# Eighth input block split first, the last blocks' final additions placed between root steps, and a fourth input tile, in a hybrid attention layer

## The chip, the cores and the metric

The kernel runs on one core of a Trainium2 chip. The core has a matmul engine (TensorE, PE in the profile, with PEld for its weight loads), VectorE (DVE), ScalarE (ACT), GpSimd (POOL) and SyncE (SP); each takes its instructions in one fixed order and waits where an instruction's inputs or its output's space aren't ready. SP and POOL mainly issue DMAs here. The metric is the device time of one execution in microseconds (us).

## The reference

One layer over 1024 tokens of width 1024: a normed projection into queries, keys, values and gates, two kinds of attention, a mix, and a gated MLP, each with a residual.

```python
h = rms_norm(x, pre_mix_g)
proj = h @ w_in                      # q, k, v of two attentions, gates
...                                  # differential and dilated attention
mix = (g_a * ya + g_b * yb) @ w_mix_out
x = x + rms_norm(mix, post_mix_g)
h = rms_norm(x, pre_ffn_g)
u = causal_depthwise_conv(h @ w_up, conv_w, conv_b)
gate, val = jnp.split(u, 2, axis=-1)
y = (gelu(gate) * val) @ w_down
x = x + rms_norm(y, post_ffn_g)
```

Everything is float32. Only the very first stage (the value columns of `proj`) and the very last (the product with `w_down`, its norm and the residual) are touched by the change.

## The kernel before, in words

**Precision.** A float32 operand is held as a high and a low part (`whi`/`wlo` for weights, `xh`/`xl` for x): ACT writes the high part, DVE subtracts it from the source to get the low part (L146, L367), and `mm3` makes three matmuls (L155 to L157), high by high, high by low, low by high.

**The first stage (values).** The products of x by the value weights `w_v` are computed by a Strassen-like scheme with seven products per half of the columns, named p1 to p7, each over four k steps and four token blocks of 128. Its operands are blocks of x^T and sums of such blocks. x^T comes in eight tiles `xt` of 128 x 1024, in the order `K_FIRST = (4, 0, 5, 1, 6, 2, 7, 3)`; the pool has six buffers for them (`XT_BUFS`), so the seventh (`xt_245`) and the eighth tile (`xt_256`, rows K = 3) can be loaded only when the first tiles are done with. `split_x` (L369) splits one half of a tile: ACT writes `xh` (L371), DVE `xl`. `sums_x(k, low, high)` (L374) makes the sum operands t1 to t4 of one k from two tiles: some seven ACT and ten DVE steps, among them the last reader of a tile, the DVE step that writes `cos` (L367; the sums are formed in the buffers called `sin` and `cos`). `sums_x(0)` and `sums_x(1)` are called in the loop over the tiles after j = 5 and j = 7, `sums_x(2)` after the loop, `sums_x(3)` after the first eight steps of the product. `ready_v(n)` splits the weights of a step n, `step_v(n)` issues its matmuls, and after a product's last k step `take_v` (L490) evacuates the four accumulators, some of them by an ACT copy to `yv` (L505). The next product in the same banks can start only after that.

**The norm's rows.** From step 14 on `norm_x` (L397) loads the eight row blocks of x by POOL (`rows`, L404, 512 KB each) into four big buffers, tagged `kk`, `ang`, `sin`, `cos` in turn, and sums their squares by ACT (L401, one step of 128 x 1024, in place). The third block (`rows_670`) takes the `sin` buffer, which `sums_x(3)` has used before: its last reader there is the DVE step `t3l<-sin`, so POOL's load waits for that.

**The order.** The program is traced, and a scheduler fixes each engine's order ahead of time by its own model of costs and by priorities: `tc.high_priority(offset)` moves work forward, `tc.issue_after(ins)` keeps what is traced inside it behind an instruction on its engine, without a wait.

**The last stage.** The last product, p4 of the product with `w_down`, is made in two ways: its first four of eleven f steps go over all four token blocks, then each block m finishes its last seven by itself (L1680 on), so that PE ends the blocks one after the other. While it does, `finish` (L1617) normalises and adds the first four row blocks (tile `x2` of 128 x 1024 from `x2_d`, L1607, then DVE L1619 and L1620, then the output DMA). After each block m of the second four come: `take` (DVE, L329, from the accumulator), `sum_squares` (ACT, L1603), a product with gpost (DVE, L1686, in place, so it waits for the square to have read), `rsqrt_row` (L183: DVE `r1v`, ACT square root `r1y`, then four small DVE steps with `r1w` as the result), and for each half a DVE step L1689, `x2 = y * r + x2`, and an output DMA. The tile `x2` has three buffers: its eight loads go over SP's queue, and the fourth and later ones wait for an earlier output DMA.

Of the kernel before, what the change touches and what calls it, by code (L numbers as in the profile page):

```python
# [15 lines left out]
F32 = mybir.dt.float32  # L16
# [3 lines left out]
ALU = mybir.AluOpType  # L20
# [67 lines left out]
def trunk(ctx: ExitStack, tc: tile.TileContext, a, out):  # L88
# [90 lines left out]
        nc.vector.tensor_scalar(y, y, 1.0 / f, None, op0=ALU.mult)  # L179
        return y  # L180

    def rsqrt_row(x, y):

        v, r, w = (tiny.tile([P, 1], F32, tag="r1" + c, name="r1" + c) for c in "vyw")
        if y is None:
            nc.vector.tensor_scalar(v, x, EPS * D, None, op0=ALU.add)
        else:
            nc.vector.tensor_scalar(v, x, y, EPS * D, op0=ALU.add, op1=ALU.add)
        nc.scalar.activation(r, v, AF.Sqrt, scale=1.0 / D)
        nc.vector.reciprocal(r, r)  # L190

        nc.vector.tensor_scalar(w, r, r, v, op0=ALU.mult, op1=ALU.mult)
        nc.vector.tensor_scalar(w, w, -3.0 * D, r, op0=ALU.add, op1=ALU.mult)
        return w
# [63 lines left out]
    @contextmanager  # L258
    def behind_marks():

        with ExitStack() as stack:
            for ins in marks.values():
                stack.enter_context(tc.issue_after(ins))
            yield

    def later(n, fn, ahead=30):

# [57 lines left out]
    def f32(v):  # L325
        return v.bitcast(F32)
# [39 lines left out]
    def plus(out, x, g, y, op):  # L366
        nc.vector.scalar_tensor_tensor(out, x, g, y, op0=ALU.mult, op1=op)  # L367

    def split_x(k, sl, src):  # L369
        g = gpre[:, k : k + 1]  # L370
        nc.scalar.activation(xh[:, k, sl], src, AF.Copy, scale=g)  # L371
        plus(xl[:, k, sl], src, g, f32(xh[:, k, sl]), ALU.subtract)

    def sums_x(k, low, high):  # L374

# [69 lines left out]
    with ExitStack() as st_y:  # L445
# [94 lines left out]
        def step_v(n):  # L540
            p, i, k = steps_v[n]
            x = xs_of[p]
            if p in ("p1", "p2", "p5") and k == 0:
                left = p == "p1"
                banks[left] = ([psum() for _ in range(3)] + [psum(F32, ps_o, "o")] if left else
                               [psum(F32, q, t) for q, t in ((ps_s, "s"), (pt, "pt")) for _ in range(2)])
            use = banks[p in ("p1", "p6", "p7", "p4")]
            wh, wl = ready.pop(n)
            for m in range(4):
                tk = slice(m * P, (m + 1) * P)  # L550
                mm3(use[m], x[0][:, k, tk], x[1][:, k, tk], wh, wl, k == 0 and p in ("p1", "p2", "p5"), k == 3, p in ("p6", "p7", "p4", "p3"))
            if k < 3:
                return
            with tc.high_priority(offset=80):
                for m in range(4):
                    take_v(p, i, m, use[m])
            if p == "p7" and i == 0:
                for m in range(4):
                    tt(quarter[3, 0][m], banks[False][m], quarter[3, 0][m], ALU.add)

        with ExitStack() as st0:
# [18 lines left out]
            for j in range(KC):  # L580
                fetch_v(j)
                parts = (512,) if j else (128, 384)
                load_x(j, 0, parts)
                if j > 1:
                    load_x(j - 2, 1)
                if j == 0:
                    ready_v(j, 256)
                c = 0
                for w in parts:
                    split_x(K_FIRST[j], slice(c, c + w), xts[j][:, c : c + w])  # L590
                    c += w
                if j:
                    ready_v(j)
                if j in (5, 7):
                    sums_x(j // 2 - 2, xts[j - 4], xts[j - 5])
            load_x(6, 1)
            load_x(7, 1)
            sums_x(2, xts[5], xts[4])
            dma(cols, a["cols"])
            dma(ghead, a["diff_head_g"])  # L600
            nc.vector.tensor_scalar(ghead, ghead, 1.0 - LAM_INIT, None, op0=ALU.mult)
# [1 line left out]
                fetch_v(n)  # L603
            for n in range(8):
                step_v(n)
            for n in range(8, 10):
                ready_v(n)
            sums_x(3, xts[7], xts[6])
            for n in range(10, 12):
                ready_v(n)  # L610
# [992 lines left out]
        nc.scalar.activation(sq, y, AF.Square, accum_out=to)  # L1603

    def load_x2(r):
        x2 = norms.tile([P, D], F32, tag="x2", name="x2", bufs=3)
        dma(x2, x2_d[r * P : (r + 1) * P, :])  # L1607
        return x2

# [22 lines left out]
    for n, (p, f) in enumerate(steps):  # L1632
# [39 lines left out]
        if p == "p4" and f < 4:  # L1672
            if f == 0:
                for m in range(4):
                    sum_squares(ys[m][:, :512], s4[:, 0, m : m + 1])
                norm_first()
            finish(f)
    for m in range(4):
        rows = slice((4 + m) * P, (5 + m) * P)
        x2 = load_x2(4 + m)  # L1680
        for f in range(NH - LAST, NH):
            product(6 * NH + f, m)
        take("p4", m, banks[m])
        c21 = ys[4 + m][:, :512]
        sum_squares(c21, sums[m][:, 0:1])
        nc.vector.tensor_tensor(c21, c21, gpost2[:, :512], op=ALU.mult)  # L1686
        r = rsqrt_row(sums[m][:, 0:1], sums[m][:, 1:2])
        for sl in halves():
            nc.vector.scalar_tensor_tensor(x2[:, sl], ys[4 + m][:, sl], r, x2[:, sl], op0=ALU.mult, op1=ALU.add)  # L1689
            dma(out[rows, sl], x2[:, sl])  # L1690


def units(w, rows, cols):
# [49 lines left out]
```

## Time and profile before

| what | value |
|---|---|
| median of 3 runs | 1696.98 us (1696.39 to 1697.29) |
| the profiled execution | 1697.3 us, its span in the profile 1695.3 us |
| TensorE | 8078 matmuls, busy 1682.1 us (99%), mean granted clock 0.998 |
| VectorE | 1333.5 us (79%) |
| ScalarE | 891.8 us (53%) |
| GpSimd | 106.3 us (6%) |
| moved by DMA | 216.41 MB, mean 128 GB/s |

A row of the timeline has start, duration, engine, source line, operation, what is written and read with its shape, and in brackets how long the engine had been idle and for whom. A number in a name (`rows_670`) tells buffers apart; the profile leaves these numbers out, the orders below keep them. The durations that the trace gives for a DVE or ACT step contain the start of the next one, so the distance of two starts is shorter than the duration. A DMA issue on SP or POOL shows the time of issue; the landing is given apart.

### The profile page before, as it was taken

Reading aid. Unit: us, or ns where it says so; the run is one execution under the profiler, and the core shown is the slowest. Engines: PE = TensorE matmul, PEld = TensorE weight load, DVE = VectorE, ACT = ScalarE, POOL = GpSimd, SP = SyncE. Lnnn points to the kernel's source line nnn. Section 1 sums busy time; section 2 is a strip of 40 time slices with the busy share of each in tenths; the row PEclk is TensorE's granted clock in tenths of the full one; section 3 lists DMA queues with packets and bytes.
Section 4 is the critical chain, followed back from the end, with each engine's and each line's share of the span. In section 5 each row is a group of like instructions: output and inputs, shape, how many; then the busy total and the mean of one; then the engine's idle time right before and its main releaser. Section 6 shows DMA issues by size and latency. Waiting matters only on the chain.

```text
span 1695.3 us, 22960 instructions
## 1 busy us (share of the span) xinstructions
PE 1682.1 (99%) x8078; PEld 1410.0 (83%) x8078; DVE 1333.5 (79%) x2445; ACT 891.8 (53%) x1663; POOL 106.3 (6%) x174
## 2 busy tenths in 40 slices
PE   9999999999999999999999999999999999999997
PEld 7888888888888888888888888888888888888886
DVE  8795686877776766677756865899999989799967
ACT  7643575656454776666653533464444445355453
POOL 0031000000000000000123400300000000000000
PEclk9999999999999999999999999999999999999999
DMA  8677311214112213233585631132222222296524
GB/s 266 234 253 235 99 60 62 86 59 119 50 63 81 70 53 108 86 112 119 200 285 186 203 118 63 38 106 92 95 81 75 98 83 88 95 343 214 193 75 161
DMA packets 104451, 216.41 MB, mean 128 GB/s; under 512 B 12992, under 2 KB 22144, under 8 KB 104336
## 3 DMA queue, kind: packets, MB, share of 16 engines
q1 hardware_dynamic: 89296, 171.28, 30.5%
q0 software_dynamic: 10288, 35.28, 6.1%
q10 hardware_dynamic: 4752, 8.39, 1.3%
q8 instruction: 63, 1.03, 0.3%
q14 instruction: 52, 0.43, 0.1%
HBM read 167.05 MB, written 47.86 MB: 127 GB/s over the span
## 4 chain that ended last, share of the span: by engine, by line
PE 97%; DMA 2%; DVE 1%; ACT 1%; issue 0%; SPq 0%; DVEq 0%
PE acc L155 22%; PE acc L156 22%; PE acc L157 22%; PE acc L1578 3%; PE acc L1579 3%; PE acc L1577 3%; PE o L710 2%; PE pt L697 2%; PE acc L1258 2%; PE acc L1256 2%; PE acc L1257 2%; PE o L713 1%; PE s L156 1%; PE s L157 1%; PE s L155 1%; PE s L768 1%
## 5 line engine op out<-in xcount | busy, mean ns | idle before, releaser
L156 PE MATMUL acc<-xh,wlo 128*128 128x512 f32 x768 | 303.2, 395 | 0.0
L157 PE MATMUL acc<-xl,whi 128*128 128x512 f32 x768 | 303.1, 395 | 0.0
L155 PE MATMUL acc<-xh,whi 128*128 128x512 f32 x768 | 303.0, 395 | 0.0
L149 ACT ACTIVATE whi<-raw 128x512 fp32r<-128x512 f32 (+1 forms) x252 | 156.1, 626 | 170.3 <-PE acc L157 88.1
L146 DVE TENSOR_TENSOR wlo<-raw,whi 128x512 fp32r<-128x512 f32 (+1 forms) x252 | 178.8, 717 | 40.4 <-ACT whi L149 34.7
L156 PEld LDWEIGHTS acc<-xh,wlo 128*128 128x128 f32 x768 | 144.4, 188 | 27.8
L157 PEld LDWEIGHTS acc<-xl,whi 128*128 128x128 f32 x768 | 144.5, 188 | 27.5
L155 PEld LDWEIGHTS acc<-xh,whi 128*128 128x128 f32 x768 | 144.4, 188 | 27.3
L155 PE MATMUL acc<-mh,whi 128*128 128x512 f32 x400 | 155.8, 390 | 0.3 <-ACT mh L149 0.3
L156 PE MATMUL acc<-mh,wlo 128*128 128x512 f32 x400 | 155.6, 389 | 0.0
L157 PE MATMUL acc<-ml,whi 128*128 128x512 f32 x400 | 155.3, 389 | 0.0
L684 ACT ACTIVATE t<-acc 64x512 f32<-64x512 f32 (+1 forms) x160 | 94.7, 592 | 55.3 <-PE acc L157 53.3
L1454 DVE TENSOR_TENSOR u<-acc,u 128x512 f32<-128x512 f32 x133 | 91.3, 691 | 20.3 <-PE acc L157 20.1
L149 ACT ACTIVATE whi<-s 128x512 fp32r<-128x512 f32 x76 | 46.9, 627 | 102.3 <-PE acc L157 88.1
L685 DVE TENSOR_TENSOR t<-acc,cos 128x512 f32<-128x512 f32 x64 | 44.1, 690 | 67.1 <-ACT t L684 63.5
L155 PEld LDWEIGHTS acc<-mh,whi 128*128 128x128 f32 x400 | 75.1, 188 | 16.0 <-ACT mh L149 0.5
L156 PEld LDWEIGHTS acc<-mh,wlo 128*128 128x128 f32 x400 | 75.1, 188 | 15.6
L157 PEld LDWEIGHTS acc<-ml,whi 128*128 128x128 f32 x400 | 75.1, 188 | 15.5
L1578 PE MATMUL acc<-whi,wlo 128*128 128x512 f32 x220 | 77.6, 390 | 0.0
L1577 PE MATMUL acc<-whi 128*128 128x512 f32 x220 | 76.4, 389 | 0.0
L1579 PE MATMUL acc<-wlo,whi 128*128 128x512 f32 x220 | 73.2, 390 | 0.0
L777 ACT ACTIVATE s<-s,mx 128x896 f32<-128x896 f32 (+7 forms) x64 | 49.4, 772 | 36.9 <-DVE mx L770 21.0
(387 smaller groups left out, 3941.6 us busy)
## 6 DMA issues: line engine op xcount, KB each, us to landing
raw<-in_w_in SPq DMA_DIRECT2D x96, 256.0 KB, 2.9
raw<-in_w_up SPq DMA_DIRECT2D x88, 256.0 KB, 2.8
raw<-in_w_v SPq DMA_DIRECT2D x71, 256.0 KB, 4.7
raw<-c_d SPq DMA_DIRECT2D x48, 256.0 KB, 3.8
c_d<-c SPq DMA_DIRECT2D x22, 512.0 KB, 2.7
raw<-in_w_down SPq DMA_DIRECT2D x37, 256.0 KB, 4.1
v_d<-yv POOLq DMA_DIRECT2D x32, 256.0 KB, 4.5
gt_d<-gate ACTq DMA_DIRECT2D x32, 256.0 KB, 2.1
```

What stands on the lines that cost most here:

```text
L146: eng.tensor_tensor(lo, src, hi.bitcast(F32), op=ALU.subtract)
L149: copy = nc.scalar.activation(hi, src, AF.Copy)
L155: nc.tensor.matmul(o, sh, mh, start=first, stop=False, skip_group_check=on)
L156: nc.tensor.matmul(o, sl, mh, start=False, stop=False, skip_group_check=on)
L157: nc.tensor.matmul(o, sh, ml, start=False, stop=last, skip_group_check=on)
L684: nc.scalar.activation(t1[dst], ps[src], AF.Copy)
L685: nc.vector.tensor_tensor(t2, ps, cos[:, sl], op=ALU.mult)
L777: exp = nc.scalar.activation(sc[c][:, :w], sc[c][:, :w], AF.Exp, bias=mx[:, c, 0:1], scale=-1.0, accum_out=den[:, c : c + 1])
L1454: nc.vector.tensor_tensor(to, made(p), x, op=ALU.add)
L1577: nc.tensor.matmul(banks[m], gh[:, tk], wh, start=f == 0, stop=False)
L1578: nc.tensor.matmul(banks[m], gl[:, tk], wh, start=False, stop=False)
L1579: nc.tensor.matmul(banks[m], gh[:, tk], wl, start=False, stop=f == NH - 1)
```

## The change

(a) `split_x` returns its ScalarE instruction. `sums_x(0)`, `sums_x(1)`, `sums_x(2)`, the preparation of steps 8 and 9 (now at high priority) and the evacuations stand behind the split of the block before them, the last three behind the eighth block's. (b) The final additions of block m in the last stage are put between the root steps of block m + 1, one ahead of `r1v` and one behind the square root, and the ACT and DVE steps of the four blocks are kept in sequence by `in_turn`. (c) `x2` has four buffers instead of three.

```diff
-    def rsqrt_row(x, y):
+    def rsqrt_row(x, y, between=()):
+        ready = list(between)
         v, r, w = (tiny.tile([P, 1], F32, tag="r1" + c, name="r1" + c) for c in "vyw")
+        if ready:
+            ready.pop(0)()
...
         nc.scalar.activation(r, v, AF.Sqrt, scale=1.0 / D)
+        if ready:
+            ready.pop(0)()
         nc.vector.reciprocal(r, r)
...
+    tail = {}
+    @contextmanager
+    def in_turn():
+        with ExitStack() as stack:
+            for ins in tail.values():
+                stack.enter_context(tc.issue_after(ins))
+            last = nc.cur_bb.bb.instructions[-1]
+            yield
+            traced = nc.cur_bb.bb.instructions
+            start = next(k for k in reversed(range(len(traced))) if traced[k] is last) + 1
+            for ins in traced[start:]:
+                if ins.engine in (nc.scalar.engine, nc.vector.engine):
+                    tail[str(ins.engine)] = ins
...
     def split_x(k, sl, src):
         g = gpre[:, k : k + 1]
-        nc.scalar.activation(xh[:, k, sl], src, AF.Copy, scale=g)
+        copy = nc.scalar.activation(xh[:, k, sl], src, AF.Copy, scale=g)
         plus(xl[:, k, sl], src, g, f32(xh[:, k, sl]), ALU.subtract)
+        return copy.ins
...
-            with tc.high_priority(offset=80):
+            with tc.high_priority(offset=80), tc.issue_after(split_last[0]):
                 for m in range(4):
                     take_v(p, i, m, use[m])
...
                 for w in parts:
-                    split_x(K_FIRST[j], slice(c, c + w), xts[j][:, c : c + w])
+                    got_x = split_x(K_FIRST[j], slice(c, c + w), xts[j][:, c : c + w])
                     c += w
...
                 if j in (5, 7):
-                    sums_x(j // 2 - 2, xts[j - 4], xts[j - 5])
+                    with tc.issue_after(got_x):
+                        sums_x(j // 2 - 2, xts[j - 4], xts[j - 5])
+            split_last = [got_x]
             load_x(6, 1)
             load_x(7, 1)
-            sums_x(2, xts[5], xts[4])
+            with tc.issue_after(got_x):
+                sums_x(2, xts[5], xts[4])
...
-            for n in range(8, 10):
-                ready_v(n)
+            with tc.issue_after(got_x), tc.high_priority(offset=160):
+                for n in range(8, 10):
+                    ready_v(n)
...
-        x2 = norms.tile([P, D], F32, tag="x2", name="x2", bufs=3)
+        x2 = norms.tile([P, D], F32, tag="x2", name="x2", bufs=4)
...
+    late = []
+    tail.clear()
+    def send(m, half, r, x2):
+        sl, rows = halves()[half], slice((4 + m) * P, (5 + m) * P)
+        nc.vector.scalar_tensor_tensor(x2[:, sl], ys[4 + m][:, sl], r, x2[:, sl], op0=ALU.mult, op1=ALU.add)
+        dma(out[rows, sl], x2[:, sl])
...
-        take("p4", m, banks[m])
         c21 = ys[4 + m][:, :512]
-        sum_squares(c21, sums[m][:, 0:1])
-        nc.vector.tensor_tensor(c21, c21, gpost2[:, :512], op=ALU.mult)
-        r = rsqrt_row(sums[m][:, 0:1], sums[m][:, 1:2])
-        for sl in halves():
-            nc.vector.scalar_tensor_tensor(x2[:, sl], ys[4 + m][:, sl], r, x2[:, sl], op0=ALU.mult, op1=ALU.add)
-            dma(out[rows, sl], x2[:, sl])
+        with in_turn():
+            take("p4", m, banks[m])
+        with in_turn():
+            sum_squares(c21, sums[m][:, 0:1])
+            nc.vector.tensor_tensor(c21, c21, gpost2[:, :512], op=ALU.mult)
+        with in_turn():
+            r = rsqrt_row(sums[m][:, 0:1], sums[m][:, 1:2], late)
+        late[:] = [functools.partial(send, m, half, r, x2) for half in range(2)]
+    for fn in late:
+        fn()
```

No instruction is added or dropped. The orders differ in the first 130 us and in the last 40 us; PE's order differs in the first stage alone. Three places follow; line numbers behind the change are about 20 to 30 higher than before.

**SP, loads of the first stage.** `xt_245` and `xt_256` are the seventh and eighth input tile, `raw_...` are value weights. Before:

```order
L570 DMA xt_217<-in_xT 128x512
L599 DMA edge_58<-in_cols 128x8
L570 DMA xt_245<-in_xT 128x512 x2
L600 DMA ghead_84<-in_diff_head_g 128x1
L126 DMA raw_304<-in_w_v 128x512
L126 DMA raw_306<-in_w_v 128x512
L126 DMA raw_308<-in_w_v 128x512
L570 DMA xt_256<-in_xT 128x512 x2
L126 DMA raw_310<-in_w_v 128x512
```

After:

```order
L592 DMA xt_217<-in_xT 128x512
L624 DMA edge_58<-in_cols 128x8
L625 DMA ghead_84<-in_diff_head_g 128x1
L126 DMA raw_304<-in_w_v 128x512
L126 DMA raw_306<-in_w_v 128x512
L126 DMA raw_308<-in_w_v 128x512
L126 DMA raw_310<-in_w_v 128x512
L592 DMA xt_245<-in_xT 128x512 x2
L126 DMA raw_312<-in_w_v 128x512
L126 DMA raw_314<-in_w_v 128x512
L592 DMA xt_256<-in_xT 128x512 x2
```

The seventh tile's load now stands behind four weight loads, the eighth's behind three more.

**DVE and ACT, where the norm's third row block comes in.** On DVE, `t3l_119<-sin_440` is the last reader of the buffer that `rows_670` gets; `xl_99<-t1_127` and `t4l_121` belong to the same sums (k = 3), `wlo_...` and `raw_...` are weights. Before:

```order
L367 SCALAR_TENSOR_TENSOR xl_99<-t1_127,xh_98 128x512
L146 TENSOR_TENSOR t3l_119<-sin_440,t3h_118 128x512
L146 TENSOR_TENSOR t4l_121<-cos_285,t4h_120 128x512
L146 TENSOR_TENSOR wlo_621<-wz_136,whi_620 128x512
L146 TENSOR_TENSOR wlo_644<-wz_136,whi_643 128x512
L146 TENSOR_TENSOR wlo_667<-raw_594,whi_666 128x512
L329 TENSOR_TENSOR raw_638<-raw_638,raw_640 128x512
L146 TENSOR_TENSOR wlo_688<-raw_615,whi_687 128x512
L367 SCALAR_TENSOR_TENSOR cos_441<-xt_245,edge_58,t1_127 128x512
L329 TENSOR_TENSOR raw_661<-raw_661,raw_663 128x512
```

After:

```order
L146 TENSOR_TENSOR wlo_621<-wz_136,whi_620 128x512
L388 SCALAR_TENSOR_TENSOR t1_127<-xt_256,edge_58,sin_440 128x512
L388 SCALAR_TENSOR_TENSOR sin_440<-xt_245,edge_58,sin_440 128x512
L146 TENSOR_TENSOR wlo_644<-wz_136,whi_643 128x512
L146 TENSOR_TENSOR wlo_667<-raw_594,whi_666 128x512
L350 TENSOR_TENSOR raw_638<-raw_638,raw_640 128x512
L146 TENSOR_TENSOR t4l_121<-cos_285,t4h_120 128x512
L146 TENSOR_TENSOR wlo_688<-raw_615,whi_687 128x512
L350 TENSOR_TENSOR raw_661<-raw_661,raw_663 128x512
L388 SCALAR_TENSOR_TENSOR xl_99<-t1_127,xh_98 128x512
L146 TENSOR_TENSOR t3l_119<-sin_440,t3h_118 128x512
L388 SCALAR_TENSOR_TENSOR cos_441<-xt_245,edge_58,t1_127 128x512
```

Seven DVE steps that stood behind `t3l_119<-sin_440` (`t4l_121`, four `wlo`, two `raw`) now stand ahead of it. On ACT, `rows_670` is that row block's square, `yv_469` the evacuation of the accumulator `acc_336`. Before:

```order
L401 ACTIVATE rows_670,ssx_128<-rows_670 128x1024
L149 ACTIVATE t4h_120<-cos_441 128x512
L149 ACTIVATE whi_756<-raw_684 128x512
L505 ACTIVATE yv_469<-acc_336 128x512
L505 ACTIVATE yv_470<-acc_337 128x512
```

After:

```order
L149 ACTIVATE whi_756<-raw_684 128x512
L149 ACTIVATE t4h_120<-cos_441 128x512
L423 ACTIVATE rows_670,ssx_128<-rows_670 128x1024
L527 ACTIVATE yv_469<-acc_336 128x512
L527 ACTIVATE yv_470<-acc_337 128x512
```

The square now stands directly ahead of the evacuations.

**DVE, the last two blocks of the last stage.** `y_13980` and `y_13981` are the blocks m = 2 and m = 3, with `x2_15951` and `x2_15990` their input tiles before, `x2_15947` and `x2_15986` after; `y_13979` is m = 1. Before:

```order
L1689 SCALAR_TENSOR_TENSOR x2_15912<-y_13979,r1w_15941,x2_15912 128x512 x2
L1686 TENSOR_TENSOR y_13980<-y_13980,gpost2_13973 128x512
L188 TENSOR_SCALAR r1v_15978<-sd_13998 128x1
L190 RECIPROCAL r1y_15979<-r1y_15979 128x1
L192 TENSOR_SCALAR r1w_15980<-r1y_15979,r1v_15978 128x1
L329 TENSOR_TENSOR y_13981<-acc_15755,y_13981 128x512
L193 TENSOR_SCALAR r1w_15980<-r1w_15980,r1y_15979 128x1
L1689 SCALAR_TENSOR_TENSOR x2_15951<-y_13980,r1w_15980,x2_15951 128x512 x2
L1686 TENSOR_TENSOR y_13981<-y_13981,gpost2_13973 128x512
L188 TENSOR_SCALAR r1v_16017<-sd_13999 128x1
L190 RECIPROCAL r1y_16018<-r1y_16018 128x1
```

After:

```order
L350 TENSOR_TENSOR y_13981<-acc_15755,y_13981 128x512
L1722 TENSOR_TENSOR y_13981<-y_13981,gpost2_13973 128x512
L1710 SCALAR_TENSOR_TENSOR x2_15947<-y_13980,r1w_15976,x2_15947 128x512
L191 TENSOR_SCALAR r1v_16013<-sd_13999 128x1
L1710 SCALAR_TENSOR_TENSOR x2_15947<-y_13980,r1w_15976,x2_15947 128x512
L195 RECIPROCAL r1y_16014<-r1y_16014 128x1
L197 TENSOR_SCALAR r1w_16015<-r1y_16014,r1v_16013 128x1
L198 TENSOR_SCALAR r1w_16015<-r1w_16015,r1y_16014 128x1
L1710 SCALAR_TENSOR_TENSOR x2_15986<-y_13981,r1w_16015,x2_15986 128x512 x2
```

Before, block m = 2's two additions stood between the take of m = 3 and its product with gpost; now they stand behind that product, one on each side of `r1v`.

More of the change, by code (lines that the diff above doesn't have):

```diff
@@ L1677, in trunk @@
             finish(f)
+    late = []
[4 more added lines that the diff above has]
+        dma(out[rows, sl], x2[:, sl])
     for m in range(4):
-        rows = slice((4 + m) * P, (5 + m) * P)
         x2 = load_x2(4 + m)
```

## The prediction

> **What bounds the kernel now.** The page comes first.
>
> ```profile
> span 1695.3 us, 22960 instructions
> PE 1682.1 (99%) x8078; PEld 1410.0 (83%) x8078; DVE 1333.5 (79%) x2445; ACT 891.8 (53%) x1663; POOL 106.3 (6%) x174
> ```
>
> PE is busy for all but 13.2 us, and no matmul is added or dropped, so the change can only move those gaps or make new ones. The waits of PE up to 130 us name one gap of size after the start, and the timeline shows it:
>
> ```profile
> PE acc L155 <- ACT xh L371: 1.8, 2, 1.4
> ...
> 23.79 0.76 DVE L367 SCALAR_TENSOR_TENSOR t<-xt,edge,sin 128x512 f32<-128x512 f32 x1
> 24.59 0.63 ACT L382 ACTIVATE xh<-t 128x512 fp32r<-128x512 f32 x1
> 25.12 0.71 ACT L371 ACTIVATE xh<-xt,edge 128x512 fp32r<-128x512 f32 x1
> 25.88 0.98 PE L155 MATMUL acc<-whi,xh 128*128 128x512 f32 x3 [1.39 <-ACT xh L371]
> ```
>
> PE stands 1.39 us for the eighth block's split, which waits behind a sums step that itself waits for DVE. The other end is the tail, seen in the chain of waits and the timeline:
>
> ```profile
> 1686.29 3.82 DMA x<-x_d
> ...
> 1675.09 0.69 DVE L329 TENSOR_TENSOR y<-pt,y 128x512 f32<-128x512 f32 x1 [2.72 <-PE pt L1579]
> 1682.49 0.68 DVE L329 TENSOR_TENSOR y<-acc,y 128x512 f32<-128x512 f32 x1
> ...
> 1685.88 0.68 DVE L329 TENSOR_TENSOR y<-acc,y 128x512 f32<-128x512 f32 x1
> 1686.65 0.63 ACT L1603 ACTIVATE sq<-y 128x512 f32<-128x512 f32 x1 [1.20 <-DVE y L329]
> 1686.72 1.42 DVE L1689 SCALAR_TENSOR_TENSOR x<-y,r1w,x 128x512 f32<-128x512 f32 x2
> 1688.05 0.69 DVE L1686 TENSOR_TENSOR y<-y,gpost 128x512 f32<-128x512 f32 x1
> 1688.65 0.21 DVE L188 TENSOR_SCALAR r1v<-sd 128x1 f32<-128x1 f32 x1
> 1690.60 1.42 DVE L1689 SCALAR_TENSOR_TENSOR x<-y,r1w,x 128x512 f32<-128x512 f32 x2 [0.74 <-DMA x<-x_d]
> ```
>
> The first row is a load of an input tile, L329 the takes of the first, third and fourth block. From the last take (1685.88) to the end of the last addition (1692.02) pass 6.14 us, 0.74 of them waiting for the input tile's load. What matters is how much room DVE and ACT have between these ends:
>
> ```profile
> 10.00:24.00 14.00, 14.00 (x63) 11.49 (x62) 13.99 (x23) 13.59 (x24) 0.00 (x0) 1.00 1.02 362
> 40.00:60.00 20.00, 20.00 (x90) 16.34 (x89) 20.00 (x34) 12.32 (x22) 1.59 (x3) 1.00 0.59 193
> 60.00:80.00 20.00, 20.00 (x90) 16.57 (x89) 11.46 (x23) 15.85 (x31) 2.12 (x4) 1.00 0.88 311
> ```
>
> In each row of this table of windows the numbers behind the length are PE, PEld, DVE, ACT and POOL. DVE is full from 10 to 60 us and has 8.5 us to spare only from 60 to 80. A step that DVE does later before 60 us stays late until then.
>
> **The change part by part.** *The first sums, behind the sixth tile.* In the trace DVE does three steps of `sums_x(0)` before 16.3 us, while the tiles still come in:
>
> ```profile
> 13.67 0.75 DVE L367 SCALAR_TENSOR_TENSOR t<-xt,edge,sin 128x512 f32<-128x512 f32 x1
> 14.34 0.75 DVE L367 SCALAR_TENSOR_TENSOR sin<-xt,edge,sin 128x512 f32<-128x512 f32 x1
> ...
> 15.61 0.75 DVE L367 SCALAR_TENSOR_TENSOR cos<-xt,edge,t 128x512 f32<-128x512 f32 x1
> 16.27 0.75 DVE L367 SCALAR_TENSOR_TENSOR xl<-xt,edge,xh 128x512 fp32r<-128x512 f32 x1
> ...
> 18.19 0.75 DVE L367 SCALAR_TENSOR_TENSOR cos<-xt,edge,cos 128x512 f32<-128x512 f32 x1
> ```
>
> Now they may only start behind the sixth tile's split. The splits that remain there come at the pace of the loads, so DVE has a hole of 3 x 0.67 = 2.0 us (the starts' distance, 14.34 - 13.67), and everything behind is 2.0 late until DVE has room.
>
> *The eighth tile.* Its buffer is freed by the last `cos` step above (18.19), behind which SP issued the load at 19.75. In the new order four steps of 0.60 to 0.66 and a small one (0.16) more stand ahead of that step: 18.19 + 2.5 + 0.16 + 2.0 = 22.9, its end 23.6, and the load goes out then. Landing takes 4.8 us by that load's own row below, 3.3 by the lighter loads between 40 and 52 us:
>
> ```profile
> 19.75 0.80 SPq L570 DMA_DIRECT2D xt<-in_xT  x2
> DMA to landing us min/median/max: 4.8/4.8/4.8
> raw<-in_w_v SPq DMA_DIRECT2D x7, 256.0 KB, 3.3
> ```
>
> I take 3.3, since the weights now go ahead of it on SP and little is in flight: 26.9, split by 27.7. So the block whose split is put first arrives 2.5 us later than now. PE has more matmuls of other blocks ahead of it in its new order; I estimate this stage between -1.4 (the gap goes) and +0.6, at +0.5. It isn't added to what follows: the later wait is for an event on other engines and swallows it.
>
> *The third row block of the norm.* This is the main term.
>
> ```profile
> 52.99 0.69 DVE L146 TENSOR_TENSOR t3l<-sin,t3h 128x512 fp32r<-128x512 f32 x1
> 53.99 1.09 POOL L404 DMA_DIRECT2D rows<-in_x  x2 [23.31 <-DVE t3l L146]
> 59.73 0.69 DVE L146 TENSOR_TENSOR t2l<-cos,t2h 128x512 fp32r<-128x512 f32 x1
> 59.81 1.05 ACT L401 ACTIVATE rows<-rows 128x1024 f32<-128x1024 f32 x1
> 62.29 1.56 ACT L505 ACTIVATE yv<-acc 128x512 f32<-128x512 f32 x3
> 61.57 0.39 PE L156 MATMUL acc<-whi,t2l 128*128 128x512 f32 x1
> 63.38 0.39 PE L155 MATMUL acc<-whi,t3h 128*128 128x512 f32 x1
> DMA to landing us min/median/max: 4.1/5.0/6.9
> rows<-in_x POOLq DMA_DIRECT2D x3, 512.0 KB, 6.5
> ```
>
> `t3l` frees the buffer, POOL issues the load 1.00 us after its start, ACT squares the rows, and ACT's evacuation frees the bank for PE's next product. Today the square runs at 59.81, well ahead of the evacuation, which ends (at a third of 1.56 and a little) about 62.9, 0.5 before PE needs it. Now seven DVE steps have moved ahead of `t3l`: 7 x 0.60 to 0.66 = 4.35, and 2.0 of lag: start 52.99 + 6.35 = 59.34, issue 60.34. The eight loads of this kind land after 4.1 to 6.9 us; the three issued between 58 and 63 us have a median of 6.5 and the shortest 6.3. I take 6.3, since this issue falls into that stretch: 66.64. The square now stands directly ahead of the evacuation: 1.05 for it and about 0.6 for the evacuation give 68.3. PE's 63.38 becomes 68.3: **+4.9**. At 4.1 it is +2.7, at 6.9 +5.5. The Trainium skill's page "DMA: Bandwidth & Descriptors", section on the anatomy of one DMA (the GpSimd path), gives a fixed 2.0 us and the bytes at 436 GB/s, by which I estimate 3.2 us for 512 KB and +1.8 in place of +4.9. No load of these rows came in under 4.1 us in this trace.
>
> The DVE lag alone would also reach PE: `t2l` is one step further back, 59.73 + 2.0 + 0.6 = 62.4, done 63.1, where PE's first use stood at 61.57: +1.6, which lies inside the 4.9. Behind 68 us DVE has its 8.5 us of room, and what it does later is less late than PE is, so I find no further loss, and nothing that gives the time back: PE is busy throughout.
>
> *The tail.* With four `x2` buffers the last load goes out before the last additions, so the 0.74 us goes. But the new order of a block puts take, square, product with gpost and then the former block's two additions in a row. The product must wait until the square has read: the square starts 0.77 after the take (1686.65 - 1685.88) and takes 0.63, then comes 0.60 for the product, and DVE has nothing else in between. From `r1v` to the first addition pass 1.21 without the load's wait (1690.60 - 0.74 - 1688.65), of which ACT's root is about 0.5; an addition of 0.66 now covers it. A block with the former's additions takes 0.77 + 0.63 + 0.60 + 2 x 0.66 + 0.16 + 0.7 = 4.2 on DVE, the first block, without any, 0.77 + 0.63 + 0.60 + 1.21 = 3.2. From the first take at 1675.09 the third comes at 1682.5, as now, but the last at 1686.7, 0.8 behind now, since the second block's additions lie ahead of it. Its own first addition follows at 1690.9, and 1.4 for both end at 1692.3, against 1692.0. I put +0.2 on it; the ends are -0.7 (the wait goes, nothing else changes) and +0.6 (the last four output DMAs bunch up, and with them the landing at the end).
>
> **The sum.** Against the profiled execution's 1697.3 us (span 1695.3): +4.9 + 0.2 = 1702.4. The median of the runs shown is 0.3 lower, so 1702.1 for a median. 0.2%, 3.4 us, is about what a measurement of this kernel can tell from no change.
>
> **Rivals.** *The load is quicker.* With less on the DMA queues than in the old stretch it lands in 3.3 us (the median of the 256 KB loads between 40 and 52 us, half its size) to 4.1, and only +1.9 to +2.7 remain, with the DVE lag's +1.6 as a floor: about 1699.4. For it: SP's queue has been moved, and the weight loads there may fall elsewhere. Against it: the DMA share of 0.88 from 60 to 80 us.
>
> *The long wait slows PE.* PE would stand from about 65.0 (its last matmuls of the product before, 63.38 + 1.6) to 68.3, 3.3 us. At the start of the program matmuls come slower until PE has worked for a while:
>
> ```profile
> 6.10 0.63 PE L156 MATMUL s<-whi,xl 128*128 128x512 f32 x1
> 6.53 0.60 PE L157 MATMUL s<-wlo,xh 128*128 128x512 f32 x1
> 7.67 0.40 PE L156 MATMUL s<-whi,xl 128*128 128x512 f32 x1
> 7.90 0.39 PE L157 MATMUL s<-wlo,xh 128*128 128x512 f32 x1
> ```
>
> 0.43 us apart first, 0.23 later. If that comes back, half of the slow time is lost: between 0.8 (5.3 to 7.0 us at the start) and 3.0 (all from 1.2 to 7.2), I take 1.9: 1704.0. Against it: behind the 1.39 us wait at 25.88 the matmuls are at full pace. The Trainium skill's page "TensorE: Matmul & The Clock Gate", in its part on the clock gate's two states, has this rule: an idle window of about 3.4 us halves the clock and as long a busy one restores it, by which I estimate 1.7 us. A wait of 3.3 us is at its edge, and no such wait lies in this trace.
>
> *It becomes faster.* This needs the `sin` buffer to come free earlier than I read, by the sums step before (k = 2), so that POOL's load lands before about 61.2 us, the point from which the square no longer holds up the evacuation. If DVE then also keeps up, so that the eighth block is in by 24.5, PE's gap of 1.39 goes, and at the tail 0.74: 1697.0 - 2.1 = 1694.9. Against it: POOL's row names `t3l` as what it waited for, for 23.31 us, and DVE has no empty place before 60 us.
>
> **How the numbers follow.** Forecast 0.65, quicker load 0.18, slow PE 0.08, faster 0.09. The predicted time is the forecast's, 1702.1. The range goes from 1698.6 (the floor of the quicker load, +1.6) to 1704.1 (slow PE, or the load at 6.9 with +0.6 at the tail) and leaves out the faster case and the ends. Within 0.2% (up to 1700.4) lie the quicker load, most of the faster case and some 0.07 of the forecast (a load near the median of 5.0): 0.32 in all; faster than 1693.6 only a part of the faster case, 0.03; slower 0.65.
>
> **What would show it.** Right: in the profile after, PE waits for ACT `yv` L527 for some 3 us at 65 to 68; POOL's third load goes out at about 60 behind `t3l`; the eighth tile lands near 27; DVE idles about 2 us between 10 and 17; the last addition ends as long after PE's last matmul as before. Wrong: PE's first product at t3 starts within 2 us of 63.4, or the tail behind PE's last matmul is shorter by over a microsecond, or a PE wait of over a microsecond lies between 70 and 1660 us.

## The result, and the profile after

| kernel | median, us | runs | ratio to before, with its 95% interval |
|---|---|---|---|
| before | 1697.22 (1696.39 to 1698.0) | 6 | |
| changed | 1703.94 (1701.11 to 1705.98) | 6 | 1.0039 (1.0029 to 1.005) |
| changed, a second time (an experiment below) | 1702.0 (1701.7 to 1705.29) | 5 | 1.0036 (1.0023 to 1.0048) |

The change makes the kernel 0.4% slower, some 5 to 7 us. Its runs also lie further apart than those of before. The profiled execution took 1701.91 us, one of the shorter ones, with this page:

```profile
span 1699.9 us, 22955 instructions
PE 1682.9 (99%) x8078; PEld 1408.4 (83%) x8078; DVE 1334.8 (79%) x2445; ACT 891.2 (52%) x1663; POOL 108.8 (6%) x174
```

The span is 4.6 us longer with 0.8 us more busy time on PE, so PE stands still for longer. The waits of PE name the places (in total, times, the longest):

```profile
PE s L155 <- ACT xh L392: 1.8, 2, 1.7
...
PE acc L155 <- ACT xh L392: 1.2, 2, 0.7
PE acc L155 <- ACT yv L527: 1.1, 1, 1.1
PE acc L156 <- DVE t2l L146: 0.5, 1, 0.5
PE s L155 <- ACT yv L536: 0.3, 1, 0.3
```

Between 20 and 130 us, where one wait of 1.39 us stood before the change, there are now five (1.65, 0.69, 0.35, 0.51 and 1.12), and the timeline puts them in order, with the loads and steps behind them:

```profile
23.78 0.80 SPq L592 DMA_DIRECT2D xt<-in_xT  x2
24.92 0.73 PE L155 MATMUL s<-whi,xh 128*128 128x512 f32 x2 [1.65 <-ACT xh L392]
28.63 0.96 PE L155 MATMUL acc<-whi,xh 128*128 128x512 f32 x3 [0.69 <-ACT xh L392]
...
60.10 0.68 DVE L146 TENSOR_TENSOR t3l<-sin,t3h 128x512 fp32r<-128x512 f32 x1
61.07 1.19 POOL L426 DMA_DIRECT2D rows<-in_x  x2 [4.10 <-DVE t3l L146]
63.23 0.68 DVE L146 TENSOR_TENSOR t2l<-cos,t2h 128x512 fp32r<-128x512 f32 x1
63.97 0.50 PE L156 MATMUL acc<-whi,t2l 128*128 128x512 f32 x1 [0.51 <-DVE t2l L146]
65.50 1.06 ACT L423 ACTIVATE rows<-rows 128x1024 f32<-128x1024 f32 x1 [1.53 <-DMA rows<-in_x]
66.56 1.55 ACT L527 ACTIVATE yv<-acc 128x512 f32<-128x512 f32 x3
67.19 0.50 PE L155 MATMUL acc<-whi,t3h 128*128 128x512 f32 x1 [1.12 <-ACT yv L527]
```

The load of the third row block goes out behind `t3l` at 61.07, ACT waits 1.53 us for it with the evacuations standing behind, and PE's first product with t3 starts at 67.19 where it started at 63.38: 3.8 us late. From there to PE's last matmul (start 1689.04, before 1685.09) PE stays 3.8 to 4.0 late. VectorE's hole shows in the windows:

```profile
10.00:24.00 14.00, 13.27 (x59) 10.62 (x57) 11.79 (x20) 8.65 (x14) 0.00 (x0) 1.00 1.01 358
```

11.79 us busy of 14, where it was 13.99. The tail of the changed kernel, with the last block's take first:

```profile
1690.75 0.68 DVE L350 TENSOR_TENSOR y<-acc,y 128x512 f32<-128x512 f32 x1
1691.52 0.63 ACT L1629 ACTIVATE sq<-y 128x512 f32<-128x512 f32 x1 [1.75 <-DVE y L350]
1692.28 0.69 DVE L1722 TENSOR_TENSOR y<-y,gpost 128x512 f32<-128x512 f32 x1 [0.85 <-ACT sq L1629]
1692.88 0.74 DVE L1710 SCALAR_TENSOR_TENSOR x<-y,r1w,x 128x512 f32<-128x512 f32 x1
1693.67 0.74 DVE L1710 SCALAR_TENSOR_TENSOR x<-y,r1w,x 128x512 f32<-128x512 f32 x1
1695.31 1.41 DVE L1710 SCALAR_TENSOR_TENSOR x<-y,r1w,x 128x512 f32<-128x512 f32 x2 [0.26 <-DVE r1w L198]
```

DVE waits 0.85 us for the square with nothing else to do. The wait of the last addition for its tile is gone. The last addition ends at 1696.72, 7.68 us behind the start of PE's last matmul; before, it ended at 1692.01, 6.92 us behind a start at 1685.09. So of the 4.6 us, 3.95 come in ahead of PE's last matmul, and 0.65 behind it.

### The profile page after: what moved, and what is told of

Read it like the earlier page. It is cut to its first block, busy times and chain, and to the rows that moved or that the text cites. A ratio compares the mean times of both kernels' runs of the same rounds, so it can differ in the third digit from the quotient of the medians.

```text
span 1699.9 us, 22955 instructions
## 1 busy us (share of the span) xinstructions
PE 1682.9 (99%) x8078; PEld 1408.4 (83%) x8078; DVE 1334.8 (79%) x2445; ACT 891.2 (52%) x1663; POOL 108.8 (6%) x174
## 4 chain that ended last, share of the span: by engine, by line
PE 95%; DVE 2%; DMA 2%; ACT 1%; issue 0%; DVEq 0%; SPq 0%; ACTq 0%
PE acc L155 22%; PE acc L156 21%; PE acc L157 21%; PE acc L1605 3%; PE acc L1604 3%; PE acc L1603 3%; PE o L736 2%; PE pt L723 2%; PE acc L1284 2%; PE acc L1282 2%; PE acc L1283 2%; PE o L739 1%; PE pt L1603 1%; PE pt L1604 1%; PE pt L1605 1%; PE s L794 1%
```

## The experiments

Twelve kernels, one of them the changed kernel again (e5), in three groups (e1 to e4, e5 to e8, e9 to e12); those of a group ran on one chip beside runs of the kernel before (its medians there 1697.38, 1697.29 and 1697.52). "t3 start" is the start of PE's first product with t3 in the profiled execution (63.38 before), "tail" the time from the start of PE's last matmul to the end of the last addition (6.92 before). Starts in single profiles differ from the very beginning: PE's 23rd matmul, which starts at 9.65 in the profile of before, starts between 8.93 and 9.78 in the others. "Late" therefore counts from that matmul to the t3 start and gives the difference to before (53.73); for the changed kernel's first profile it is 4.1.

| experiment | median, us | ratio (95%) | t3 start | late | tail |
|---|---|---|---|---|---|
| e1 changed first stage alone | 1701.31 (1700.56 to 1703.57) | 1.0026 (1.0017 to 1.0035) | 65.88 | 2.9 | 6.58 |
| e2 changed last stage alone | 1697.24 (1696.15 to 1698.05, and one run of 6322.2) | 0.9998 (0.9989 to 1.0007) | 62.51 | -0.2 | 7.45 |
| e3 first two sums free | 1699.82 (1698.03 to 1701.57) | 1.0014 (1.0005 to 1.0023) | 63.27 | -0.2 | 7.44 |
| e4 square behind evacuations | 1702.66 (1700.87 to 1704.87) | 1.0032 (1.0021 to 1.0042) | 65.44 | 2.4 | 7.45 |
| e5 changed again | 1702.0 (1701.7 to 1705.29) | 1.0036 (1.0023 to 1.0048) | 66.85 | 4.1 | 7.67 |
| e6 square and lambda steps off | 1700.98 (1699.45 to 1702.41) | 1.0021 (1.0012 to 1.003) | 65.36 | 2.7 | 7.68 |
| e7 gpost behind the root | 1694.94 (1694.53 to 1696.44) | 0.9988 (0.9979 to 0.9997) | 62.95 | 0.1 | 5.24 |
| e8 e7, and the eighth split first | 1694.54 (1693.87 to 1695.06) | 0.9985 (0.9976 to 0.9994) | 62.06 | -1.0 | 5.25 |
| e9 four tiles alone | 1695.16 (1694.53 to 1697.39) | 0.9988 (0.9979 to 0.9996) | 62.46 | -0.2 | 5.55 |
| e10 seven tiles of x transposed | 1703.01 (1700.1 to 1704.55) | 1.0031 (1.002 to 1.0041) | 65.75 | 2.8 | 7.44 |
| e11 lambda steps off alone | 1702.11 (1700.83 to 1703.78) | 1.0029 (1.0019 to 1.0039) | 66.47 | 3.6 | 7.67 |
| e12 first sums held, alone | 1701.64 (1699.39 to 1703.14) | 1.0022 (1.0013 to 1.0031) | 67.94 | 5.3 | 5.47 |

### e1 and e2: each stage alone

e1 has the changed `split_x`, `sums_x` calls, `take_v` and `ready_v`, with the old last stage; e2 has the new last stage, with each `issue_after` of the first stage, and the raised priority of steps 8 and 9, taken out:

```diff
-                    with tc.issue_after(got_x):
+                    with nullcontext():
                         sums_x(j // 2 - 2, xts[j - 4], xts[j - 5])
```

> The changed first stage with the last stage of before (three input tiles, additions behind their own block). Theory (the loss sits in the first stage: DVE is late, and the square of the third row block, waiting for its load, holds up the evacuation): PE's last matmul is 4 us later than before, as in the changed kernel, and the time is 1697.2 + 4 to 6 = 1701 to 1703.5; the runs spread over 3 us or more. Rival (the last stage carries a good part of the loss): under 1700.

> The first stage of before with the changed last stage (additions between root steps, four input tiles). Theory (the new order of the last stage takes back what the fourth tile gives): the end of the last addition comes 0.4 to 0.8 us later behind PE's last matmul than before, time 1697.6 to 1698.2. Rival (the fourth tile's 0.74 us is a gain): 1696.4 or less.

e1 takes 1701.31, e2 1697.24: the loss is in the first stage. As a median the new last stage costs nothing, a little less than its theory had; its tail is 7.45 in the profile, 0.5 longer than before as expected, which lies within what the comparison can tell. e1's runs spread over 3 us as expected. In e1's profile the wait for the evacuation is short (0.30), and PE is 2.5 us late at the t3 start, but new waits follow at 80 us and make it 4.2: the wait for a load that I had named wasn't the only one. e5, the changed kernel once more, was expected at 1701.5 to 1704 if the first stage alone costs the time, and at 1703.5 or more if the last stage adds 2 us in its company; it took 1702.0, near e1.

### e3: the first two sums free

```diff
-                    with tc.issue_after(got_x):
+                    with nullcontext():
                         sums_x(j // 2 - 2, xts[j - 4], xts[j - 5])
```

with all the rest of the change kept.

> The changed kernel, but the first two sums are again not held behind the split of the tile before; the third sums, the steps 8 and 9 and the evacuations stay behind the eighth tile's split. Theory (holding the first sums back makes DVE 2 us late, and with it the eighth tile and the third row block): DVE's third t3 part is back near 54 us, no wait for the evacuation at 67, the first stage costs -0.5 to +0.7, with the last stage's +0.7 the time is 1697.4 to 1698.8. Rival (the evacuations and steps 8 and 9 held back make the loss): 1701 or more.

The first stage is back: `t3l` at 52.49 (expected near 54; before 52.99, changed 60.10), the t3 start at 63.27. PE's 351st matmul starts at 85.94 us in e3 and at 86.05 in before, so the whole loss of the first 86 us is gone. But the median is 1699.82, a microsecond above what was expected, and the profile shows a place, another evacuation at 136 us behind a weight split that waits for a sum of loads:

```profile
134.00 0.69 DVE L350 TENSOR_TENSOR raw<-raw 128x512 f32<-128x512 f32 x1 [3.85 <-DMA raw<-in_w_v]
134.79 0.63 ACT L149 ACTIVATE whi<-raw 128x512 fp32r<-128x512 f32 x1 [5.70 <-DVE raw L350]
136.66 0.51 PE L155 MATMUL acc<-whi,t3h 128*128 128x512 f32 x1 [1.58 <-ACT yv L525]
```

e7, whose first stage is that of before, also waits at this place in its profile (0.9 us), so e3's wait at 136 us is not proved to come from the change. PE's last matmul is 2.9 us later than in before (1687.99 against 1685.09), all of it made behind 86 us. Holding the first sums makes some 2 to 4 us of the loss; the rest of it stays open between the other held steps and this wait.

### e4, e6 and e11: the two loads ahead of ScalarE's work

e4 moves the square of the third row block behind the evacuations:

```diff
-        if m > 2:
-            t = rows_x[m - 3]
-            with behind_marks():
-                nc.scalar.activation(t, t, AF.Square, accum_out=ssx[:, m - 3 : m - 2])
+        for q in {5: (), 6: (2, 3)}.get(m, (m - 3,) if m > 2 else ()):
+            t = rows_x[q]
+            with behind_marks(), tc.issue_after(took[-1]) if m == 6 else nullcontext():
+                nc.scalar.activation(t, t, AF.Square, accum_out=ssx[:, q : q + 1])
```

(`took` holds the evacuations.) e11 moves the lambda steps instead, and e6 does both; `made_v` keeps the split of each step n:

```diff
-                lambda_scale()
+                with tc.issue_after(made_v[27][1]), tc.issue_after(made_v[28][0]):
+                    lambda_scale()
```

> The changed kernel with one step moved on ScalarE: the square of the third row block stands behind the four evacuations instead of ahead of them; its load is issued as in the changed kernel. Theory: PE's wait for the evacuation (1.1 us in the profiled run) goes, the first stage costs about 2.8 us in the profile, the median falls by 2 us or more to 1701 to 1702, and since the runs differ by when that load lands, they now lie within 2 us. Rival (the evacuation is late for another reason, or the next square takes the place): 1703 to 1705 with a spread of 4 us.

> The changed kernel with two things moved back on ScalarE and VectorE: the square of the third row block behind the evacuations (as in the run before), and the lambda steps, which wait for the load of diff_lambda, behind the weight splits whi_798 to whi_845 and their low parts, where they were before the change. Theory (two waits for loads in a fixed order, the second taking the first one's place): neither holds PE any more, only VectorE's lag of about 2 us is left (t2 part): PE is about 2 us late at 85 us and the median is 1699 to 1700.5. Rival (a third wait takes the place, the loads are late by themselves): 1702 or more.

> The changed kernel with the lambda steps alone moved back behind the weight splits; the square of the third row block stays ahead of the evacuations. Theory (either of the two waits is enough to set the time, the earlier one covers the later): 1701 to 1703, PE 3.3 us late or more at 68 us and nothing new behind it. Rival (the lambda steps were the real hold-up): 1699.5 to 1700.5.

In e4 the wait for the evacuation goes and the t3 start is at 65.44 instead of 67.19, but the median stays at 1702.66 with a spread of 4 us. That lies between the ranges of theory and rival; as the rival had it, another wait takes the place, though it isn't the next square's, and the spread isn't made by that one load. It is shown by the rows of e4:

```profile
77.16 0.29 DVE L350 TENSOR_TENSOR raw<-raw 128x128 f32<-128x128 f32 x1 [0.70 <-DMA raw<-in_diff_lambda]
77.81 0.20 ACT L464 ACTIVATE ls<-ls 128x2 f32<-128x2 f32 x1 [5.86 <-DVE ls L463]
77.92 1.14 ACT L149 ACTIVATE whi<-raw 128x512 fp32r<-128x512 f32 x2
78.58 0.50 PE L155 MATMUL acc<-whi,t4h 128*128 128x512 f32 x1 [0.74 <-ACT whi L149]
81.70 0.50 PE L155 MATMUL s<-whi,xh 128*128 128x512 f32 x1 [1.19 <-ACT whi L149]
```

The exponential of lambda (`ls`) stands ahead of two weight splits in the changed order, behind them in the order of before; ACT waits 5.86 us for it, because DVE's sum waits for the load of `diff_lambda`. With the lambda steps alone moved (e11) the first wait covers it: 1702.11, t3 start 66.47. With both moved (e6), neither wait is left; behind 20 us the main waits of PE are these and one of 0.58 us at 23 us:

```profile
27.78 0.96 PE L157 MATMUL acc<-whi,xh 128*128 128x512 f32 x3 [1.32 <-ACT xh L394]
...
63.41 0.50 PE L158 MATMUL acc<-whi,t2l 128*128 128x512 f32 x1 [0.61 <-DVE t2l L148]
...
907.95 0.50 PE L157 MATMUL acc<-oah,whi 128*128 128x512 f32 x1 [0.80 <-DVE ya L1223]
```

The t3 start is 2.0 later than in before, 2.7 if the different start is allowed for, and 81 us are passed without a new wait. It is not VectorE's lag at `t2l` alone, as the theory had it: up to 32 us PE also waits 0.58 and 1.32 us for the late input tiles and 0.35 for an evacuation, where before it waited 1.39. The median is 1700.98, half a microsecond above its range; the profile adds a wait for the attention's `ya` at 908 us, which the profiles of before and of the changed kernel don't have (e12 has one of 0.47) and whose cause stays open. So the two loads together are worth 1 to 3 us, and more than half of the loss stands without them.

### e10: seven tiles

`XT_BUFS` is 7 instead of 6 in the changed kernel.

> The changed kernel with seven buffers for the tiles of x transposed instead of six, so that the seventh tile's load waits for no buffer and the eighth's for the first tile of all. Theory (VectorE's late start of the sums makes the loss, the buffers only pass it on): the eighth tile lands some 2 us sooner than in the changed kernel, but VectorE still reaches the third t3 part near 59 us, PE is 3 us late or more at 68 us, time 1700.5 to 1703. Rival (the late eighth tile is the root): 1699 or less.

The eighth tile's load goes out at 19.96 instead of 23.78 and PE passes the blocks without the wait (2.0 us ahead of before at the start of its products, 23.84 against 25.88; 0.45 of this is the earlier start of the program). The gain is lost again by 66 us:

```profile
58.02 0.50 PE L156 MATMUL s<-whi,xl 128*128 128x512 f32 x1 [0.54 <-DVE xl L388]
61.28 0.97 PE L155 MATMUL acc<-whi,t2h 128*128 128x512 f32 x3 [1.14 <-ACT t2h L149]
65.75 0.50 PE L155 MATMUL acc<-whi,t3h 128*128 128x512 f32 x1 [1.29 <-ACT yv L527]
```

`t3l` runs at 57.88 (expected near 59). PE waits for VectorE's sums wherever it would have been early; the median is 1703.01, at the upper end of the theory's range. The late eighth tile is not the root.

### e12: the first sums held, and nothing else

```diff
-                    with nullcontext():
+                    with tc.issue_after(got_x) if j == 5 else nullcontext():
                         sums_x(j // 2 - 2, xts[j - 4], xts[j - 5])
```

on top of e7.

> The best last stage (product with gpost behind the root) with the first stage of before, but the first sums alone held behind the sixth tile's split; second and third sums, steps 8 and 9 and the evacuations as before the change. Theory (this one line makes VectorE 2 us late, the eighth tile's load 3 to 4 us late, and leaves the two loads standing in front): 3 to 5 us more than with the first sums free (1694.94): 1698 to 1700. Rival (the other lines are needed for the loss): 1696 or less.

1701.64 against 1694.94, 6.7 us from one line, more than expected (5.0 between the two profiled executions, 1701.42 and 1696.44). Part of it is a rival of the prediction that no other profile shows:

```profile
23.99 0.72 PE L155 MATMUL s<-whi,xh 128*128 128x512 f32 x2 [1.16 <-ACT xh L392]
27.99 1.65 PE L155 MATMUL acc<-whi,xh 128*128 128x512 f32 x3 [2.80 <-ACT xh L392]
29.43 0.63 PE L155 MATMUL o<-whi,xh 128*128 128x512 f32 x1
29.86 0.63 PE L156 MATMUL s<-whi,xl 128*128 128x512 f32 x1
...
33.27 0.56 PE L155 MATMUL s<-whi,xh 128*128 128x512 f32 x1
33.67 0.40 PE L156 MATMUL s<-whi,xl 128*128 128x512 f32 x1
33.91 0.40 PE L157 MATMUL s<-wlo,xh 128*128 128x512 f32 x1
```

and in the windows, where the last three numbers are the granted clock, the DMA share and GB/s:

```profile
26.00:27.00 1.00, 0.00 (x0) 0.00 (x0) 1.00 (x2) 0.00 (x0) 0.00 (x0) 0.90 0.93 344
27.00:33.00 6.00, 5.01 (x12) 3.96 (x13) 6.00 (x11) 3.52 (x6) 0.00 (x0) 0.50 0.83 232
33.00:34.00 1.00, 1.00 (x5) 0.79 (x4) 1.00 (x2) 1.00 (x3) 0.69 (x1) 0.69 0.90 139
```

Behind waits of 1.16 and 2.80 us the matmuls start 0.43 us apart instead of 0.23 until 33.3. The granted clock is 0.90, 0.50 and 0.69 in these windows, so it was halved from about 26.8 to 33.6. PE is 2.1 us late when it starts again and 4.7 late when the pace is back (33.91, where the same matmul starts at 29.23 in before): 2.6 us for the slow stretch. From that matmul to the t3 start pass 34.03 us, 34.15 in before. So the third row block adds nothing here; e12 shows that the one hold is enough for a loss, and this loss takes another way than the changed kernel's.

### e7, e8 and e9: the last stage, and a kernel that is faster than both

e7 takes e2 and puts the product with gpost behind the root, where DVE has no wait:

```diff
-            nc.vector.tensor_tensor(c21, c21, gpost2[:, :512], op=ALU.mult)
         with in_turn():
-            r = rsqrt_row(sums[m][:, 0:1], sums[m][:, 1:2], late)
+            r = rsqrt_row(sums[m][:, 0:1], sums[m][:, 1:2], (late or [lambda: None])[:1] + [scaled])
```

(`scaled` issues the second addition and then that product.) e9 is the kernel before with `bufs=4` for `x2` and nothing else. e8 is e7 with one ACT step of the second sums held behind the eighth tile's split:

```diff
-        nc.scalar.activation(b12[0][:, k], nt1, AF.Copy, scale=-1.0)
+        with tc.issue_after(first) if first is not None else nullcontext():
+            nc.scalar.activation(b12[0][:, k], nt1, AF.Copy, scale=-1.0)
```

> The first stage of before; the last stage of the change, but the product with gpost stands behind the square root instead of directly behind the take, so VectorE doesn't wait for the square with the former block's additions behind it. Theory (that wait in VectorE's order takes back what the fourth tile gives): the last addition ends 5.2 to 5.8 us behind PE's last matmul instead of 6.9, time 1695.6 to 1696.4. Rival (the output DMAs or the reciprocal chain set the end): 1697 to 1697.6.

> As the run above, and in the first stage one step alone is held back: ScalarE's high part of t1 in the second sums stands behind the eighth tile's split; VectorE's sums stay in the loop. Theory (the eighth split can go first without making VectorE late): PE's wait of 1.4 us at 25.9 falls to 0.8 or less and no new wait comes in, time 0.6 to 1.0 us less than the run above: 1694.8 to 1695.6. Rival (the step held back makes VectorE's sums late, and the time is given back before 130 us): equal to the run above or more.

> The kernel before with one change: four buffers for the input tiles of the last stage instead of three, the order of the steps left to itself. Theory (the last load's wait is on the path): the 0.7 us wait of the last addition for its tile goes, the last addition ends 6.2 to 6.5 us behind PE's last matmul, time 1696.4 to 1696.9. Rival (the last addition is then late for VectorE's own chain): 1697.1 to 1697.5.

All three are faster than before, and each by more than its theory gave. In the kernel before, `finish` of the fourth block waited 0.98 us for its tile and stood on DVE ahead of the second block's take:

```profile
1676.77 1.28 DVE L1620 SCALAR_TENSOR_TENSOR x<-y,r1w,x 128x1024 f32<-128x1024 f32 x1 [0.98 <-DMA x<-x_d]
1677.97 0.68 DVE L329 TENSOR_TENSOR y<-pt,y 128x512 f32<-128x512 f32 x1
```

With the fourth tile (e9) that take follows the first one:

```profile
1673.79 0.69 DVE L329 TENSOR_TENSOR y<-pt,y 128x512 f32<-128x512 f32 x1 [1.53 <-PE pt L1579]
...
1674.70 0.69 DVE L329 TENSOR_TENSOR y<-pt,y 128x512 f32<-128x512 f32 x1 [0.21 <-PE pt L1579]
```

PE's last matmul starts 1.30 us earlier in e9's profile (0.72 of it from the program's start), so against PE the second take is 2.0 us earlier; more is gone than the last addition's wait. The tail falls by 1.4 us (6.92 to 5.55), the median by 2.4, with an interval of 0.7 to 3.6. e7, with additions between the root steps, has nearly the same time as e9 without them (1694.94 and 1695.16) and a tail of 5.24 against 5.55. So the additions between the root steps are worth nothing that the medians can tell. e7's rows show what they do, with no wait behind the last block's take:

```profile
1687.07 1.41 DVE L1710 SCALAR_TENSOR_TENSOR x<-y,r1w,x 128x512 f32<-128x512 f32 x2
...
1688.39 0.21 DVE L191 TENSOR_SCALAR r1v<-sd 128x1 f32<-128x1 f32 x1
1688.51 0.68 DVE L1726 TENSOR_TENSOR y<-y,gpost 128x512 f32<-128x512 f32 x1
...
1689.86 1.41 DVE L1710 SCALAR_TENSOR_TENSOR x<-y,r1w,x 128x512 f32<-128x512 f32 x2
```

In e8 the eighth tile is split as it comes in and PE's wait shrinks from 1.39 to 0.30:

```profile
23.73 0.72 ACT L392 ACTIVATE xh<-xt,edge 128x512 fp32r<-128x512 f32 x1
24.50 0.96 PE L155 MATMUL acc<-whi,xh 128*128 128x512 f32 x3 [0.30 <-ACT xh L392]
```

The median is 1694.54, 0.4 less than e7, where 0.6 to 1.0 was expected, and the difference of the two is smaller than either interval. e8 has the lowest median here, 2.75 us below before, but can't be told from e7 and e9.

## Why the prediction was right or wrong

The direction, the stage and the chain were right, and both medians of the changed kernel (1703.94 and 1702.0) lie in the range. The terms of the sum were partly wrong and offset one another: +4.9 measured 3.8, +0.2 measured 0.76. That the second median comes so close to the forecast of 1702.1 is in part luck, since the two medians of the same kernel lie 1.9 us apart.

- *The hole.* 2.0 us were predicted from three held steps; VectorE is busy 2.2 us less between 10 and 24 us. At `t3l` the lag is 2.8 instead of 2.0 (60.10 against 59.34 forecast, seven steps and 2.0 behind 52.99). That VectorE had no empty place before 60 us was misread: between 24 and 40 us, where no window was shown, it was busy 14.83 us of 16. e3 shows that holding the first two sums is the root of the early loss: without it `t3l` is back at 52.49 and PE is not late at 86 us. e12 shows that holding the first sums alone is enough to lose as much, though by the tiles and a slow PE.
- *The eighth tile.* Forecast: load out at 23.6, split by 27.7. Measured: 23.78, and in use by PE at 28.63, since the landing took 4.1 to 4.3 us and not the 3.3 of the lighter loads. The stage cost about 1.3 us (waits of 1.65, 0.69 and 0.35 in place of 1.39), beyond my upper end of 0.6.
- *The third row block.* The mechanism came as told, in each row: `t3l`, POOL's issue behind it, the square, the evacuation, PE. The size was off. I took 6.3 us for the landing, from loads issued at the same time of the old program; it was 4.3 (61.07 to 65.4), inside the bounds of 4.1 to 6.9. PE's product came 3.8 us late and not 4.9, and PE stood only 1.1 us for the evacuation, not some 3, because the load was quicker and because the tiles and `t2l` had already made PE late. And I let this one event stand for the whole loss ("the later wait is for an event on other engines and swallows it"): e4 and e6 show that it adds only 1.4 to 1.8 us at the t3 start to a lag that is there without it.
- *No further loss behind 68 us.* In the changed kernel's profile this holds: from the t3 start to PE's last matmul pass 1621.85 us, 1621.71 before. But the reason given, VectorE's room, missed a step: the lambda steps had moved ahead of the weight splits, and the prediction doesn't mention them. Their wait is covered as long as the row block's wait comes first; in e1 and e4, where that is shorter or gone, PE waits up to 1.9 us for them.
- *The tail.* Forecast +0.2, measured +0.76 in the profile by the tail as defined above, a little over the upper end of 0.6, and nothing by the medians of e2. The chain of a block on DVE was right: the takes of e2 lie 4.2 us apart. The two terms were both too small. The fourth tile takes 1.4 us off the tail (e9) and not 0.74, for it also frees DVE ahead of the second take; the new order gives back 1.9 (7.45 of e2 against 5.55 of e9; 2.1 by the medians, of runs on two chips). The wait for the square that the prediction named, with the additions behind it, makes this: e7 moves the product away from it and has 5.24. The Trainium skill's page "DMA: Bandwidth & Descriptors", in the section on the anatomy of one DMA, would by my estimate have made the row block's landing 3.2 us; 4.3 was measured, and no row load of the changed kernel came in under 3.6.
- *The rivals.* A quicker load came in part. The slow PE did not show in the changed kernel's profile, where the longest wait is 1.65 us; it showed in e12. Whether the changed kernel's longer runs, up to 1705.98, have it, isn't shown, since they were not profiled; so it stays open whether the median of 1703.94 is the forecast's case or this rival's, whose time was 1704.0. For the rival "faster" nothing spoke.

## What to carry to other kernels

Work held back behind a late arrival, on an engine that has no room, delays everything behind it on that engine by about the time that the engine then stands idle (2.2 us idle here, 2.8 at `t3l`), and the bill comes where the next transfers wait for its buffers. In a fixed order, look for each instruction that waits for a load and stands ahead of work that TensorE needs; taking one away brings the next to light, so move them all before judging (e4, e11, e6). A buffer more and a new order in one change can cancel: try each by itself (by the medians e9 gained 2.4 us, and the order took 2.1 back).

## What the runs showed of the hardware

A wait of 1.16 us and one of 2.80 us with some 1.2 us of matmuls between them sufficed for the slow pace of 0.43 us per matmul, which lasted from 27.99 to 33.3, 5.3 us, and cost 2.6 us (e12). The granted clock had fallen to 0.50 at about 26.8, some 1.6 us into the second wait, and stayed there for about 6.8 us. Single waits of 1.39 (before) and 1.65 us (changed) didn't bring it on. The Trainium skill's page "TensorE: Matmul & The Clock Gate", in its Part 1 on the HAM clock gate, asks for an idle window of about 3.4 us; the 2.80 us here were shorter, with the other wait just ahead. At the program's start the change to the full pace comes at another time in each run: matmuls start 0.43 us apart until about 7 us in the profile of before, until about 4.2 us in that of e2.
